# Split weights kept in DRAM by the first token block, x1 and weight stores issued by Pool, and column-tile products whose tiles end one by one

## The chip, the cores and the metric

The kernel runs on one core of one Trainium2 chip. The metric is device time in microseconds of one execution. A core has TensorE (PE in the profile, with its weight loads as PEld), VectorE (DVE), ScalarE (ACT), GpSimd (POOL) and SyncE (SP, which here only issues DMAs). Each engine works off its own queue of instructions in order; semaphores order them among each other. DMAs move data between DRAM and the on-chip SBUF.

## The reference

One layer, sequence 2048, model width 1024, all in float32:

```
h = rmsnorm(x, norm1_w);  p = h @ w_in
y_ssd = ssd_mixer(p[z, xBC, dt])     # causal conv over 4 steps + silu on x, B, C; chunked scan; gate; norm
y_ml  = mlstm_mixer(p[qk, v, o, i, f])  # causal conv + silu on q, k; exponential gates; matrix memory; norm
x = x + concat(y_ssd, y_ml) @ w_out
x = x + hier_moe(rmsnorm(x, norm2_w))   # top-1 of 4 groups, top-2 of 8 experts in it, SwiGLU experts
out = rmsnorm(x, norm_f_w)
```

`w_in` is 1024 rows wide (13 products of 512 columns here, and a few gate columns), `w_out` has 2048 rows and 1024 columns.

## The kernel before, in words

The mixer goes over the sequence in four token blocks of 512 tokens (`for b in range(nblk)`, L1112), some 510 us each; after the last, from about 2100 us on, come the experts, which stream all expert weights. In each block `product` (L260) is called 13 times for `w_in` and 8 times for halves of `w_out` quarters.

A product has four accumulators of 128x512 in PSUM (`acc`). To keep float32 accuracy with a faster matmul form, each operand is a sum of a high and a low half, and a product is three passes: high by high, low by high, high by low. The activations' halves (`hh`, `hl`) are made once per block. The weights' halves are made for each product anew, by `wpieces` (L244): a piece is 256 rows by 512 columns, one DMA on SP of 512 KB into `raw` (two buffers), then for each 128 rows `split` (L233): ScalarE rounds to `whi` (L239 or L236) and VectorE subtracts to `wlo` (L240 or L237). `whi` and `wlo` have five buffers each. A `w_in` product has four pieces, a half of a `w_out` quarter two: 68 pieces per block, 272 in all. Each piece feeds 24 matmuls: 4 accumulators x 2 row groups x 3 passes, one accumulator's 6 after another's.

There are two kinds of product. Kind "t" puts tokens on the accumulators' rows; kind "c" puts columns there, so that each accumulator is one column tile, and `conv` (L282) takes each tile through the causal convolution: a copy to `craw` on ScalarE (L288), small copies of the history on Pool (L287, L289), a scaled copy (L294), three multiply-adds on VectorE (L301), a tanh (L302) and a last step on VectorE (L303), which makes `xc` (x, B and C) or `qk`. PE transposes `xc` to `tx` (L1160), and multiplies `qk` to `sp` (L1287). The scans (`ssd_scan`, L1170, and the mLSTM's) alternate between PE, VectorE, ScalarE and Pool. Seven products of a block are of kind "c".

At a block's end `x1`, the residual sum, is stored twice to DRAM: as it is (`accd`), and after Pool has multiplied it in place by `norm2_w` (`scaled`, L610) as `x1d`. `stores` (L597) issues these eight DMAs of 512 KB on SP, in the next block's start. The tile of `x1` is loaded with the next block's `x` (2 MB, L1366, on SP) when they are done with it.

The queues are not written by hand: the tile framework schedules all instructions from the dependences, the buffers (a buffer is taken again when its last reader is done) and hints such as `tc.issue_after`; `side` steps are handed out between the accumulators of a product. So an edit moves instructions far from its own lines.

The core of the split, L239 and L240:

```
A.activation(hi, src, AF.Copy, scale=w)
V.scalar_tensor_tensor(lo, src, w, hi.bitcast(F32), op0=OP.mult, op1=OP.subtract)
```

## Time and profile before

| | |
|---|---|
| median of 3 runs | 2999.13 us (2998.03 to 3005.5) |
| profiled execution | 3002.55 us |
| its span | 3000.7 us |
| mean granted clock of TensorE | 0.977 |
| PE busy | 2809.5 us, 94% |
| DVE busy | 2135.3 us, 71% |
| ACT busy | 1485.5 us, 50% |

The span is the stretch that the profiler saw; the execution's own time lies 1.85 us above it. Busy times are sums of an engine's instructions; a wait is idle time of an engine, put down to the instruction of another engine that ended it. The granted clock is TensorE's clock as the throttle let it run, as a share of full speed. SP is not counted as busy, since it only issues.

### The profile page before, as it was taken

The numbers are of one execution on the slowest core, as the hardware profiler recorded it, in microseconds if no ns is written. First come the engines' busy times: TensorE is split into PE (matmuls) and PEld (weight loads), VectorE is DVE, ScalarE is ACT, GpSimd is POOL, SyncE is SP. The second block draws the span as 40 slices with busy tenths as digits, with TensorE's granted clock in tenths as the row PEclk, the third lists the DMA queues.
The fourth block names the chain that finished last, engine by engine and source line by source line (L and its number), as shares of the span: only waits on it lengthen the run. The fifth ranks groups of instructions, "written<-read, shape, count | busy, mean of one in ns | idle before, by whom it ended". The sixth has DMA issues, their size and how long they took to land. (4 is left out here: it accounts for less than half of the span.)

```text
span 3000.7 us, 41203 instructions
## 1 busy us (share of the span) xinstructions
PE 2809.5 (94%) x13444; PEld 2226.4 (74%) x13444; DVE 2135.3 (71%) x4035; ACT 1485.5 (50%) x2326; POOL 666.8 (22%) x721
## 2 busy tenths in 40 slices
PE   7999999999999999999999999996889899999985
PEld 5778877777887777788777788785667677787763
DVE  6886487688658678856767974775787777757773
ACT  5544345454434544544445453433666666646662
POOL 1431010352101045100006510001122322412433
PEclk9999999999999999999999999997999999999997
DMA  4222322422322241232224133143998999878983
GB/s 150 70 64 92 91 78 76 145 68 75 95 71 78 84 155 57 71 99 91 65 73 152 57 99 92 54 119 135 310 321 281 311 295 302 277 238 261 302 291 95
DMA packets 228917, 438.05 MB, mean 146 GB/s; under 512 B 38218, under 2 KB 38294, under 8 KB 228641
## 3 DMA queue, kind: packets, MB, share of 16 engines
q1 hardware_dynamic: 206640, 380.88, 38.6%
q0 software_dynamic: 22000, 53.75, 6.7%
q8 instruction: 142, 2.33, 0.3%
q14 instruction: 135, 1.10, 0.1%
HBM read 400.84 MB, written 54.95 MB: 152 GB/s over the span
## 5 line engine op out<-in xcount | busy, mean ns | idle before, releaser
L643 DVE TENSOR_TENSOR lo<-mraw,hi 128x1024 fp32r<-128x1024 f32 x384 | 454.9, 1230 | 75.0 <-ACT hi L642 60.6
L239 ACT ACTIVATE whi<-raw,pcol 128x512 fp32r<-128x512 f32 x416 | 295.0, 721 | 344.0 <-PE acc L277 140.1
L240 DVE SCALAR_TENSOR_TENSOR wlo<-raw,pcol,whi 128x512 fp32r<-128x512 f32 x416 | 318.5, 781 | 201.0 <-ACT whi L239 200.2
L642 ACT CAST hi<-mraw 128x1024 fp32r<-128x1024 f32 x384 | 384.0, 1051 | 87.7 <-DMA mraw<-in_exp_w_up_dram 34.9
L275 PE MATMUL acc<-hh,whi 128*128 128x512 f32 x896 | 366.6, 410 | 0.6 <-ACT whi L239 0.6
L275 PE MATMUL acc<-hh,wlo 128*128 128x512 f32 x896 | 357.6, 401 | 8.1 <-DVE wlo L240 7.9
L275 PE MATMUL acc<-hl,whi 128*128 128x512 f32 x896 | 360.4, 402 | 0.0
L277 PE MATMUL acc<-whi,hh 128*128 128x512 f32 x768 | 311.0, 405 | 2.0 <-ACT craw L288 2.0
L277 PE MATMUL acc<-whi,hl 128*128 128x512 f32 x768 | 310.2, 404 | 0.0
L277 PE MATMUL acc<-wlo,hh 128*128 128x512 f32 x768 | 308.6, 404 | 0.0
L277 PE MATMUL acc<-whi,mh 128*128 128x512 f32 x512 | 204.5, 399 | 0.0
L275 PEld LDWEIGHTS acc<-hh,wlo 128*128 128x128 f32 x896 | 169.3, 189 | 47.0 <-DVE wlo L240 10.9
L277 PE MATMUL acc<-whi,ml 128*128 128x512 f32 x512 | 203.4, 397 | 0.0
L277 PE MATMUL acc<-wlo,mh 128*128 128x512 f32 x512 | 203.1, 398 | 0.0
L289 POOL COPY hist<-craw 128x3 f32<-128x3 f32 x112 | 39.0, 349 | 718.5 <-ACT craw L288 718.1
L275 PEld LDWEIGHTS acc<-hh,whi 128*128 128x128 f32 x896 | 170.2, 190 | 34.3 <-issue 3.5
L275 PEld LDWEIGHTS acc<-hl,whi 128*128 128x128 f32 x896 | 169.9, 190 | 32.0 <-issue 2.6
L287 POOL COPY craw<-hist 128x3 f32<-128x3 f32 x112 | 69.1, 620 | 479.4 <-DVE ir L426 360.5
L277 PEld LDWEIGHTS acc<-whi,hh 128*128 128x128 f32 x768 | 146.1, 190 | 35.7 <-ACT craw L288 3.8
L277 PEld LDWEIGHTS acc<-wlo,hh 128*128 128x128 f32 x768 | 145.7, 190 | 34.9 <-issue 1.9
L277 PEld LDWEIGHTS acc<-whi,hl 128*128 128x128 f32 x768 | 146.4, 191 | 31.8 <-issue 1.0
L809 POOL DMA_INDIRECT accd<-pv,eti x46 | 85.5, 1859 | 338.9 <-ACT hi L642 102.2
(421 smaller groups left out, 6156.8 us busy)
## 6 DMA issues: line engine op xcount, KB each, us to landing
raw<-in_w_in_dram SPq DMA_DIRECT2D x208, 512.0 KB
mraw<-in_exp_w_gate_dram SPq DMA_DIRECT2D x128, 512.0 KB
mraw<-in_exp_w_up_dram SPq DMA_DIRECT2D x128, 512.0 KB
mraw<-in_exp_w_down_dram SPq DMA_DIRECT2D x128, 512.0 KB
raw<-in_w_out_dram SPq DMA_DIRECT2D x64, 512.0 KB
xi<-in_x_dram SPq DMA_DIRECT2D x16, 512.0 KB
x<-in_x_dram SPq DMA_DIRECT2D x4, 2048.0 KB
accd<-x SPq DMA_DIRECT2D x16, 512.0 KB
```

Source lines behind the costliest of these rows:

```text
L239: A.activation(hi, src, AF.Copy, scale=w)
L240: V.scalar_tensor_tensor(lo, src, w, hi.bitcast(F32), op0=OP.mult, op1=OP.subtract)
L275: mm = PE.matmul(acc[i], b[:, s], a, start=f, stop=e)
L277: mm = PE.matmul(acc[i], a[:, s], b, start=f, stop=e)
L287: G.tensor_copy(raw[:, 0:3], hist[:, ct, :])
L289: h = G.tensor_copy(hist[:, ct, :], raw[:, T:T + 3])
L642: A.copy(hi, raw)
L643: V.tensor_tensor(lo, raw, hi.bitcast(F32), op=OP.subtract)
L809: return G.indirect_dma_start(out=accd, out_offset=bass.IndirectOffsetOnAxis(ap=en[0], axis=0), in_=pvs[t], in_offset=None, bounds_check=S ...
```

## The change

In the first block, `wpieces` loads a piece as two DMAs of 256 KB into two smaller tiles `raw` (two buffers), splits each into its part of one tile `wsp` of 128 x 2 x 2 x 512 (1 MB; three buffers), and Pool stores that tile to a DRAM tile of its own (`keep`, called one piece later). In the later blocks a piece is one DMA of 1 MB on SP from there into `wsp`, and `split` is not called. The stores of `x1` of the blocks 0 to 2 are issued by Pool; the last block's by SP. In a product of kind "c" the first half of the rows goes piece by piece as before; the last two pieces are taken together, and each accumulator gets its 12 matmuls in one go. The number of `side` steps stays the same.

```diff
--- before.py
+++ after.py
@@ -41,7 +41,6 @@
 LAST = '.H.Kd.e.PgQ.tA..B..C..ua.D.b', 'HvKwdepxgq'
 NQ = 4
 FIRST, START = 5, 10
-WB = 5
 
 
 def bc(ap, shape):
@@ -239,20 +238,36 @@
             A.activation(hi, src, AF.Copy, scale=w)
             V.scalar_tensor_tensor(lo, src, w, hi.bitcast(F32), op0=OP.mult, op1=OP.subtract)
 
-    loads = []
+    loads, kept, pend = [], {}, []
+
+    def keep():
+
+        for o, t in pend:
+            G.dma_start(o, t.bitcast(F32))
+        pend.clear()
 
     def wpieces(w, r0, nk, c0, scale=None):
 
+
         for kp in range(nk // 2):
-            raw = wp.tile([128, 2, T], F32, name="raw", tag="raw")
             a = r0 + kp * 256
-            loads.append(nc.sync.dma_start(raw, w[a:a + 256, c0:c0 + T].rearrange("(k p) c -> p k c", p=128)))
+            both = wp.tile([128, 2, 2, T], F32R, name="wsp", tag="wsp", bufs=3)
+            if (w.name, a, c0) in kept:
+                loads.append(nc.sync.dma_start(both.bitcast(F32), kept[w.name, a, c0]))
+            else:
+                raws = []
+                for k in range(2):
+                    raw = wp.tile([128, T], F32, name="raw", tag="raw")
+                    loads.append(nc.sync.dma_start(raw, w[a + k * 128:a + k * 128 + 128, c0:c0 + T]))
+                    raws.append(raw)
+                for k in range(2):
+                    sw = None if scale is None else pcol[:, scale + 2 * kp + k:scale + 2 * kp + k + 1]
+                    split(both[:, k, 0], both[:, k, 1], raws[k], sw)
+                keep()
+                o = kept[w.name, a, c0] = dram.tile([128, 2, 2, T], F32, name="w%d" % len(kept))
+                pend.append((o, both))
             for k in range(2):
-                hi = wp.tile([128, T], F32R, name="whi", tag="whi", bufs=WB)
-                lo = wp.tile([128, T], F32R, name="wlo", tag="wlo", bufs=WB)
-                sw = None if scale is None else pcol[:, scale + 2 * kp + k:scale + 2 * kp + k + 1]
-                split(hi, lo, raw[:, k, :], sw)
-                yield 2 * kp + k, hi, lo
+                yield 2 * kp + k, both[:, k, 0], both[:, k, 1]
 
     def accs():
         return [ps_acc.tile([128, T], F32, name="acc", tag="acc") for _ in range(4)]
@@ -260,10 +275,12 @@
     def product(kind, w, r0, nk, c0, src, scale=None, side=iter(())):
 
 
+
         acc = accs()
         ps = wpieces(w, r0, nk, c0, scale)
-        for k0 in range(0, nk, 2):
-            two = [next(ps), next(ps)]
+        n0 = nk // 2 if kind == "c" else nk
+        for k0 in [*range(0, n0, 2)] + [n0] * (n0 < nk):
+            two = list(islice(ps, 2 if k0 < n0 else nk - n0))
             for i in range(4):
                 s = slice(i * 128, i * 128 + 128)
                 for k, whi, wlo in two:
@@ -276,7 +293,8 @@
                         else:
                             mm = PE.matmul(acc[i], a[:, s], b, start=f, stop=e)
                 with tc.issue_after(mm.ins):
-                    next(side, None)
+                    for _ in two[::2]:
+                        next(side, None)
         return acc
 
     def conv(ps, ct, dest):
@@ -597,7 +615,7 @@
     def stores(o, t0, x1):
         for i in range(4):
             with tc.issue_after(loads[-1].ins):
-                nc.sync.dma_start(o[t0 + i * 128:t0 + i * 128 + 128, :], x1[i] if isinstance(x1, list) else x1[:, i, :])
+                (G if kept and t0 < S - T else nc.sync).dma_start(o[t0 + i * 128:t0 + i * 128 + 128, :], x1[i] if isinstance(x1, list) else x1[:, i, :])
             yield
 
     def scaled(x1, alloc):
@@ -1111,6 +1129,7 @@
     whole(gates2(*g1, gate))
     for b in range(nblk):
         t0 = b * T
+        keep()
         dt, cum, eacs, etot, dec, vs, enm = gate
 
         def hsrc(k, hs=hs):
```

Per engine, over the program: PE has the same 20394 instructions; VectorE and ScalarE have 408 fewer each; Pool issues 68 weight stores and 24 x1 stores more; SP issues 136 raw loads of half the size in place of 272, and 204 loads of 1 MB, and 24 stores fewer. The weight tiles take the same room in SBUF, 28 KB per partition (before 2 x 4 KB of `raw` and 10 x 2 KB; after 2 x 2 KB and 3 x 8 KB).

The first place is SP at the start of block 1, before. `x_604` is the tile of x1 that block 0 leaves, `x_5072` the same tile with block 1's x; in brackets is what a DMA waits for.

```order
L249 DMA raw<-in_w_in_dram 128x2x512 [waits DMAHW6_49,DVE_49]
L600 DMA accd<-x_604 128x1024
L249 DMA raw<-in_w_in_dram 128x2x512 [waits DMAHW2_49,DMAHW7_49,DVE_49,Activation_49]
L600 DMA accd<-x_604 128x1024 [waits DMAHW3_49]
L600 DMA accd<-x_604 128x1024 x2
L600 DMA x1d<-x_604 128x1024 [waits Pool_49] x2
L600 DMA x1d<-x_604 128x1024 [waits DMAHW0_49,Pool_49]
L600 DMA x1d<-x_604 128x1024 [waits DMAHW1_49,Pool_49]
L249 DMA raw<-in_w_in_dram 128x2x512 [waits DMAHW2_49,DVE_49,Activation_49]
L249 DMA raw<-in_w_in_dram 128x2x512 [waits DMAHW3_49,DVE_49]
L1366 DMA x_5072<-in_x_dram 128x4x1024 [waits DMAHW5_49,DMAHW4_49,DMAHW6_49,DMAHW1_49,DMAHW7_49,DMAHW0_49,PE_49]
```

After, at the same place: `w_...` are the kept pieces, `x_5108` is block 1's x.

```order
L256 DMA wsp<-w_429 128x2048 [waits DMASW4_49,DMASW3_49,DMASW5_49,DMASW2_49,DMASW6_49,DMASW1_49,DMASW7_49,DMASW0_49,PE_49]
L625 DMA n_5249<-in_norm_w_dram 128x512 [waits DVE_49]
L625 DMA n_5255<-in_norm_w_dram 128x512 [waits DVE_49]
L256 DMA wsp<-w_464 128x2048 [waits DMASW3_49,DMASW5_49,DMASW0_49,PE_49]
L256 DMA wsp<-w_499 128x2048 [waits DMASW4_49,DMASW6_49,DMASW1_49,PE_49]
L256 DMA wsp<-w_510 128x2048 [waits DMAHW4_49,PE_49]
L256 DMA wsp<-w_626 128x2048 [waits DMAHW7_49,DMAHW2_49,PE_49]
L1385 DMA x_5108<-in_x_dram 128x4x1024 [waits DMASW4_49,DMASW5_49,DMASW3_49,DMASW6_49,DMASW2_49,DMASW7_49,DMASW1_49,DMAHW3_49,DMASW0_49,Pool_49]
L256 DMA wsp<-w_668 128x2048 [waits DMAHW0_49,PE_49]
L256 DMA wsp<-w_717 128x2048 [waits DMAHW5_49,DMAHW1_49,PE_49]
L256 DMA wsp<-w_728 128x2048 [waits DMAHW6_49,DMAHW2_49,PE_49]
```

The stores of x1 have left SP, the load of x waits for Pool (whose queue has the eight stores, with eight multiplies between them) and stands ahead of `w_668`.

The second place is PE in block 1, in the product of X1, of kind "c", before: `acc_5523` and `acc_5524` are two of its accumulators, the other matmuls are of the first scan.

```order
L275 MATMUL acc_5523<-hh_4165,whi_5630 128x512
L275 MATMUL acc_5523<-hl_4166,whi_5630 128x512
L275 MATMUL acc_5523<-hh_4165,wlo_5631 128x512
L1205 MATMUL pS_5419<-xe_5417,bn0_5116 128x512
L1207 MATMUL pi_5421<-st_200,ct0_5046 128x512
L275 MATMUL acc_5523<-hh_4165,whi_5634 128x512
L275 MATMUL acc_5523<-hl_4166,whi_5634 128x512
L275 MATMUL acc_5523<-hh_4165,wlo_5635 128x512
L275 MATMUL acc_5524<-hh_4165,whi_5630 128x512
L275 MATMUL acc_5524<-hl_4166,whi_5630 128x512
L275 MATMUL acc_5524<-hh_4165,wlo_5631 128x512
L275 MATMUL acc_5524<-hh_4165,whi_5634 128x512
L1185 MATMUL ar_5436<-br1_208,selA_111 128x256
L275 MATMUL acc_5524<-hl_4166,whi_5634 128x512
```

After, the same product's last accumulator is `acc_5529`; `acc_5715` belongs to the next product, Z0.

```order
L292 MATMUL acc_5529<-hh_4225,wsp_5582 128x512
L292 MATMUL acc_5529<-hl_4226,wsp_5582 128x512
L292 MATMUL acc_5529<-hh_4225,wsp_5582 128x512 x2
L292 MATMUL acc_5529<-hl_4226,wsp_5582 128x512
L292 MATMUL acc_5529<-hh_4225,wsp_5582 128x512
L292 MATMUL acc_5529<-hh_4225,wsp_5584 128x512
L292 MATMUL acc_5529<-hl_4226,wsp_5584 128x512
L292 MATMUL acc_5529<-hh_4225,wsp_5584 128x512 x2
L292 MATMUL acc_5529<-hl_4226,wsp_5584 128x512
L292 MATMUL acc_5529<-hh_4225,wsp_5584 128x512
L294 MATMUL acc_5715<-wsp_5719,hh_4223 128x512
L294 MATMUL acc_5715<-wsp_5719,hl_4224 128x512
```

An accumulator gets 12 matmuls in a row where it got 6.

The third place is PE at the first transposes of X1's tiles (`tx`), in the product of Z0, before: the product of X1 stands 76 rows ahead, with much of the scan between.

```order
L277 MATMUL acc_5746<-whi_5787,hh_4163 128x512
L277 MATMUL acc_5746<-whi_5787,hl_4164 128x512
L277 MATMUL acc_5746<-wlo_5788,hh_4163 128x512
L277 MATMUL acc_5743<-whi_5817,hh_4165 128x512
L1160 MATMUL tx_5677<-ident_103,xc_5663 128x128 x4
L1160 MATMUL tx_5697<-ident_103,xc_5683 128x128 x4
L277 MATMUL acc_5743<-whi_5817,hl_4166 128x512
L277 MATMUL acc_5743<-wlo_5818,hh_4165 128x512
L277 MATMUL acc_5743<-whi_5821,hh_4165 128x512
L277 MATMUL acc_5743<-whi_5821,hl_4166 128x512
L277 MATMUL acc_5743<-wlo_5822,hh_4165 128x512
```

After, the rows that follow directly on the last rows shown above:

```order
L294 MATMUL acc_5715<-wsp_5719,hh_4223 128x512 x2
L294 MATMUL acc_5715<-wsp_5719,hl_4224 128x512
L294 MATMUL acc_5715<-wsp_5719,hh_4223 128x512
L294 MATMUL acc_5716<-wsp_5719,hh_4223 128x512
L294 MATMUL acc_5716<-wsp_5719,hl_4224 128x512
L294 MATMUL acc_5716<-wsp_5719,hh_4223 128x512 x2
L294 MATMUL acc_5716<-wsp_5719,hl_4224 128x512
L1179 MATMUL tx_5649<-ident_103,xc_5635 128x128 x4
L1179 MATMUL tx_5669<-ident_103,xc_5655 128x128 x4
L294 MATMUL acc_5716<-wsp_5719,hh_4223 128x512
L294 MATMUL acc_5717<-wsp_5719,hh_4223 128x512
L294 MATMUL acc_5717<-wsp_5719,hl_4224 128x512
```

The transposes stand 11 matmuls of Z0 behind the last of X1, and those of X1's first tile 35 product matmuls behind the end of that tile.

## Rows read from the trace of the kernel before

**Rows 1.** the page, part 1: busy time of each engine.

```profile
PE 2809.5 (94%) x13444; PEld 2226.4 (74%) x13444; DVE 2135.3 (71%) x4035; ACT 1485.5 (50%) x2326; POOL 666.8 (22%) x721
```

**Rows 2.** windows by block: length; busy (x) of PE, PEld, DVE, ACT, POOL; PEclk; DMA; GB/s.

```profile
30.00:545.00 515.00, 502.12 (x2472) 402.37 (x2470) 367.14 (x782) 238.10 (x416) 82.42 (x102) 0.99 0.26 80
545.00:1055.00 510.00, 493.94 (x2428) 396.61 (x2428) 367.32 (x812) 232.75 (x405) 105.00 (x119) 0.99 0.28 88
1055.00:1565.00 510.00, 494.25 (x2438) 396.66 (x2436) 368.21 (x813) 233.91 (x407) 104.65 (x119) 0.99 0.28 88
1565.00:2060.00 495.00, 477.91 (x2334) 385.86 (x2333) 352.03 (x776) 212.22 (x362) 104.63 (x115) 0.99 0.32 99
```

**Rows 3.** waits of PE in blocks 1 to 3: total us, times, longest.

```profile
PE acc L275 <- DVE wlo L240: 7.9, 4, 2.5
PE tx L1160 <- DVE xc L303: 7.4, 4, 2.4
PE sp L1287 <- DVE qk L303: 7.2, 3, 2.5
PE tk L1297 <- DVE mm L1289: 6.1, 6, 1.5
PE py L1199 <- DVE m L1193: 3.6, 4, 1.2
PE ar L1185 <- DVE sg L1189: 3.1, 3, 1.1
```

**Rows 4.** waits of PE in block 0: total us, times, longest.

```profile
PE tx L1160 <- DVE xc L303: 3.5, 2, 2.4
PE sp L1287 <- DVE qk L303: 2.1, 1, 2.1
```

**Rows 5.** windows just after two waits of PE, columns as in rows 2.

```profile
574.00:577.40 3.40, 3.20 (x8) 2.55 (x9) 3.34 (x6) 0.63 (x1) 1.34 (x2) 0.50 0.57 114
652.50:655.90 3.40, 3.40 (x9) 2.67 (x8) 2.48 (x4) 1.80 (x4) 2.10 (x2) 0.50 0.49 134
```

**Rows 6.** lines of the four blocks: busy us, mean ns, idle before and releaser.

```profile
L239 ACT ACTIVATE whi<-raw,pcol 128x512 fp32r<-128x512 f32 x411 | 291.6, 721 | 344.0 <-PE acc L277 140.1 <-PE acc L275 119.0 <-DMA raw<-in_w_in_dram 78.0
L240 DVE SCALAR_TENSOR_TENSOR wlo<-raw,pcol,whi 128x512 fp32r<-128x512 f32 x411 | 314.9, 781 | 201.0 <-ACT whi L239 200.2
L236 ACT CAST whi<-raw 128x512 fp32r<-128x512 f32 x128 | 78.7, 620 | 144.5 <-PE acc L277 104.7 <-DMA raw<-in_w_out_dram 21.4 <-PE acc L275 16.6
L237 DVE TENSOR_TENSOR wlo<-raw,whi 128x512 fp32r<-128x512 f32 x128 | 86.9, 687 | 89.4 <-PE acc L277 38.8 <-ACT whi L236 38.5 <-PE acc L275 12.0
```

**Rows 7.** window around one 512 KB weight load issued at 302.0, columns as in rows 2.

```profile
302.00:303.00 1.00, 1.00 (x6) 0.79 (x5) 0.00 (x0) 0.46 (x1) 0.00 (x0) 1.00 0.02 4
303.00:305.40 2.40, 2.40 (x12) 1.93 (x11) 0.69 (x1) 0.21 (x2) 0.00 (x0) 1.00 0.58 217
```

**Rows 8.** timeline of SP's queue at the start of block 1: start, us.

```profile
574.23 0.37 SPq L249 DMA_DIRECT2D raw<-in_w_in_dram  x1
574.65 2.22 SPq L600 DMA_DIRECT2D accd<-x  x3
576.91 11.18 SPq L600 DMA_DIRECT2D x1d<-x  x4
588.20 1.24 SPq L249 DMA_DIRECT2D raw<-in_w_in_dram  x2
```

**Rows 9.** window of products alone, line L277: us, PE busy (x) and PEld busy (x).

```profile
300.40:355.90 55.50, 55.50 (x239) 44.70 (x239) 1.00 0.34 104
```

**Rows 10.** lines of POOL: busy us, mean ns, idle before.

```profile
L590 POOL DMA_INDIRECT lst<-ent,sl x36 | 45.6, 1267 | 8.0 <-issue 6.4 <-DVE xc L301 1.0 <-DVE bt L301 0.5
L610 POOL TENSOR_TENSOR x<-x,n 128x512 f32<-128x512 f32 x24 | 31.9, 1358 | 10.9 <-DMA accd<-x 10.8
```

**Rows 11.** the page, part 2: GB/s in 40 slices of 75 us.

```profile
GB/s 150 70 64 92 91 78 76 145 68 75 95 71 78 84 155 57 71 99 91 65 73 152 57 99 92 54 119 135 310 321 281 311 295 302 277 238 261 302 291 95
```

**Rows 12.** window of the scan stretch of block 1, columns as in rows 2.

```profile
600.00:730.00 130.00, 123.65 (x593) 95.63 (x593) 113.72 (x209) 61.97 (x104) 59.84 (x59) 0.99 0.23 67
```

## The prediction

> **What bounds the kernel now.** I read the totals first. TensorE is busy 94% of the span, VectorE 71%, ScalarE 50% [rows 1]: nothing is gained by taking work from ScalarE or VectorE unless TensorE stops waiting for them. Then the windows by token block: in each block of some 510 us TensorE is idle 12.9, 16.1, 15.8 and 17.1 us (515.00 − 502.12, and so on) at a granted clock of 0.99 [rows 2]. The four blocks offer 62 us of idle time plus what the clock loses, and no more, since the matmuls stay the same in number and shape. The second half of the span, the experts, moves 238 to 321 GB/s where the blocks move 54 to 157 [rows 11], and the change doesn't touch it.
>
> Next, who ends the idle time in blocks 1 to 3. Six groups make 35.3 of the 48.9 us there [rows 3], and VectorE is named in all: 7.9 us for `wlo`, the low half of a split weight; 7.4 for `xc` ahead of the transposes `tx` and 7.2 for `qk` ahead of the scores `sp`, both last steps of the convolutions; 12.8 inside the two scans (`tk`, `py`, `ar`). Block 0 has the same two convolution waits, 5.6 us [rows 4]. The cause is in the scan stretch: VectorE is busy 113.72 of 130 us there, 87%, while TensorE reaches 123.65 [rows 12].
>
> [...]
>
> **The change part by part, blocks 1 to 3.** Each piece of weights arrives split. Per block 104 `whi` and 104 `wlo` of one kind and 32 of the other go: the `wlo` are 104 × 781 + 32 × 687 ns = 103 us of VectorE, the `whi` 104 × 721 + 32 × 620 ns = 95 us of ScalarE [rows 6]. VectorE falls from 367 to about 264 us per block. On the path that sets the end this is worth what TensorE waited:
> - `wlo`: all 7.9 us, since the instruction is gone.
> - `tx` and `sp`, 14.6 us: they fall due when VectorE has worked off its queue, and 103 of 367 us of that queue, over a quarter, were `wlo`. The products of kind "c" finish their four column tiles one by one, 12 matmuls apart in place of 6, so the first convolutions start earlier against the last matmul: 36, 24 and 12 matmuls ahead in place of 18, 12 and 6, at 55.50 / 239 = 0.232 us each [rows 9] 4.2 us earlier for the first. Bounds: nothing (the order only moves `tx` closer, as it did before) and all 14.6. In the new order 35 product matmuls (8.1 us) stand between the end of X1's first tile and its transposes, so I am near the upper end and take 0.8, 11.7 us.
> - the scans' 12.8 us: chains through VectorE with dependences of their own; a shorter queue shortens only the queueing part. Bounds 0 and 12.8; I take half, 6.4 us.
> - the clock: three stretches at `wlo` and four of the five others, 7 × 1.7 = 11.9 us.
>
> Together 37.9 us. In exchange come loads of 1 MB. One 512 KB load gave no data in its first microsecond (4 GB/s) and was done 3.4 us after its issue [rows 7]. A 1 MB load is then between 3.4 us (were size free) and 1.0 + 2 × 2.4 = 5.8 us. A slot comes free when TensorE is done with a piece, and there are three slots, so a load has two pieces of 24 × 0.232 = 5.6 us, 11.1 us, to land; where a "c" product holds its last two pieces together it is 1.25 pieces, 7.0 us, since both come free only during the last tile's 12 matmuls. 5.8 is under 7.0: I cost the loads at nothing inside a block. What hides them is the product itself, and it stops hiding them if something stands ahead of the load on SP.
>
> **The start of a block.** Before, SP's queue was blocked by stores: it issued one at 574.65 and the four x1d stores, each waiting for Pool's multiply, until 588.20, and two weight loads stood behind them for 13.5 us [rows 8]. Moved to Pool these leave SP. But the 2 MB load of x for this block, into the same tile, now waits for Pool's stores of it, and stands on SP ahead of the load of a later weight piece (`w_668`). Pool issues 8 stores and 8 multiplies there: no plain store is on Pool before, so I take the nearest row, 1267 ns for an indirect one, and 1358 ns per multiply [rows 10]: 8 × 2.6 = 21 us, and 3.4 us until the last landed. So the x load is issued some 24 us after the first store, and `w_668` right behind it. TensorE has five pieces ahead of that weight, 5 × 5.6 = 28 us. `w_668` lands 3.4 us after its issue if the x load costs it nothing (in time), and 6.5 us later if it goes behind all 2 MB of it (at 321 GB/s [rows 11]), some 34 us after the first store: 0 to 6 us late. Other matmuls stand between the five pieces and x shares the engines, so I take 2, in three block starts +6 us.
>
> [...] With the shorter lead of the new slots, stores left on SP would have cost up to 13.5 − 7.0 = 6.5 us at each of three starts, an estimate.
>
> **Block 0.** Nothing is removed here. Raw weights come in two loads of 256 KB into two tiles (before two tiles of 512 KB, so half the room), and Pool writes each split piece out, 68 stores of 1 MB. A raw tile's cycle is load, `whi`, `wlo`: at most 3.4 + 0.72 + 0.78 = 4.9 us [rows 6, 7] against 5.6 us of a piece, so it fits, with 0.7 us to spare and VectorE's queue not counted. A split tile is free again after its product and its store; the store is issued one piece later and has some 8 us. Per piece 0.5 MB come and 1 MB goes in 5.6 us, 283 GB/s at the most, under the 321 that the experts' part reaches [rows 11]. Bounds: 0, and every piece late by 1.5 us (VectorE two operations behind), 68 × 1.5 = 102 us. The nearest row, the cycle that fits, says near 0; I take a wait like the ones in rows 3 (2.4 + 1.7 us) twice, +8 us. The finishing of "c" tiles one by one helps `tx` and `sp` here too, 5.6 us and three stretches of clock, 5.1 us; without relief for VectorE I take half, −5.
>
> **Into the experts.** The last weight loads are 1 MB among the first expert weights: +2 us.
>
> **Sum.** −37.9 + 6 + 8 − 5 + 2 = −27 us against the profiled execution, 3002.55 us (its span is 3000.7). That execution is 3.4 us above the median of 2999.13, so the forecast is 3002.55 − 27 − 3.4 = 2972 us. Its own range: with all waits and all clock of blocks 1 to 3 gone and no cost, −49 − 8 → 2942; with half of the gain (−22) and costs of 20 → 2997.
>
> **Rivals.**
> 1. *Everything goes.* A queue on VectorE shorter by over a quarter might let every chain run ahead: all 62 us of idle time and 11 stretches of clock (19 us), −81 → 2918. For it: VectorE ends every one of the waits in rows 3. Against it: `tk`, `py` and `ar` are short waits in many places, as chains of their own make them.
> 2. *No change.* The gaps move: the order is laid out anew by a scheduler, which before put `tx` right behind the work it waits for, and SP's queue now stalls on the x load. 4 us at each of three starts, each with 1.7 us of clock, and block 0's costs of 16 use up most of the gain: 17 + 16 = 33 of 38, which is 2990 to 3008. For it: the lead of a 1 MB load is 7.0 us at worst, that of a 512 KB load before was larger. Against it: idle time that VectorE ended is twice that sum.
> 3. *Slower: block 0 is paced by the raw tiles.* With two 256 KB tiles the next load can't be issued before VectorE's `wlo`, and VectorE has 87% of its time taken in the scans [rows 12]. If two operations of 0.7 to 0.8 us are ahead of each `wlo`, the cycle is 4.9 + 1.5 = 6.4 us, and with the store's share of the DMA engines some 6.8, against 5.6: 1.2 × 68 = 82 us. −38 + 6 + 82 + 2 − 3.4 → 3051. It decides from 0.5 us per piece on, where 34 us eat the gain. Against it: in the scans a piece takes longer than 5.6 us, since other matmuls stand between, and three split tiles lend 11 us of lead.
>
> [...]
>
> **How the numbers follow.** Forecast 0.54, rival 1 0.13, rival 2 0.16, rival 3 0.17. Under 0.3%, 9 us either way (2990 to 3008), a measurement of this kernel can't be told from no change. Faster: 0.52 of the forecast, rival 1 and 0.01 of rival 2, 0.66. Same: 0.02 of the forecast and 0.13 of rival 2, 0.15. Slower: rival 3 and the rest of rival 2, 0.19. The range takes in the forecast's own, rival 2 and the near ends of the other two: 2930 to 3020.
>
> **What would show it.** Right: in the windows of blocks 1 to 3 VectorE near 264 us, TensorE's idle time near 8 us each, no wait for `wlo`, `tx` and `sp` mostly gone, a few waits for DMA `wsp` at block starts. Wrong: waits for DMA `wsp` inside the blocks (1 MB loads take over 7 us); block 0 longer than 515 us with ScalarE's `whi` waiting for `raw` (rival 3); `tx` and `sp` as long as before (the order ate the relief); the experts' part of another length.

## The result, and the profile after

The changed kernel takes 3020.32 us (median of 8 runs, 3007.56 to 3024.21) against 3001.15 us: the ratio is 1.0059, 95% interval 1.0045 to 1.0074. It is slower by 18 us by the ratio (19 by the medians) where 27 us of gain were forecast, and its runs lie further apart than those of the kernel before. Its profiled execution took 3019.25 us, its span is 3017.5.

The page's part 1 and the windows of the changed kernel, to be read against [rows 1, 2] (the windows follow its own block starts; after the times come PE, PEld, DVE, ACT, POOL, then the granted clock, DMA share, GB/s):

```profile
PE 2814.2 (93%) x13444; PEld 2227.0 (74%) x13444; DVE 1878.1 (62%) x3627; ACT 1229.1 (41%) x1918; POOL 680.4 (23%) x813
```

```profile
30.00:560.00 530.00, 498.19 (x2412) 394.84 (x2411) 364.41 (x763) 230.04 (x403) 116.31 (x171) 0.98 0.60 213
560.00:1067.00 507.00, 494.45 (x2430) 397.40 (x2429) 280.99 (x675) 147.85 (x270) 97.83 (x128) 0.99 0.46 159
1067.00:1575.00 508.00, 493.66 (x2428) 396.83 (x2427) 281.27 (x675) 147.62 (x269) 98.48 (x127) 0.99 0.46 159
1575.00:2068.00 493.00, 481.40 (x2348) 388.11 (x2348) 265.90 (x633) 131.57 (x230) 95.39 (x121) 0.99 0.48 163
```

VectorE and ScalarE lost the work that was meant to go: 257 and 256 us of busy time over the span. TensorE didn't follow. In the first block it is idle 31.8 us in place of 12.9; in the three others together 38.5 in place of 48.9.

For a ledger I divide each trace at the first product matmul of each block (there are 6528, 1632 per block). The "rest" is the span after the last. What comes before block 0, some 26 us, is left out.

| profiled execution | block 0 | block 1 | block 2 | block 3 | rest |
|---|---|---|---|---|---|
| before | 509.2 | 510.3 | 509.2 | 496.1 | 949.5 |
| changed | 533.7 | 507.1 | 508.3 | 493.0 | 948.9 |

Block 0 lost 24.5 us; the blocks that read the kept weights gained 3.2, 0.9 and 3.1. The experts' part is the same. The lengths are those of one execution each: *stores_on_act* below, which differs from the changed kernel in block 0 alone, has 505.8, 505.2 and 492.7 us in the later blocks, so a single length is good to some 3 us.

The clock has a part in it. By the clock records of the traces TensorE's stretches at a granted clock of 0.50 (these records hold 0.50 and 1.00 and no other value; in the kernel before the matmuls of a product start 0.43 us apart at 0.50, from 574.8 on, and 0.23 apart at 1.00, from 578.5 on) grew in block 0 from 10.2 to 20.5 us, which, counted as half the speed, costs 5.1 us more; the rest of the 24.5 is idle time. In blocks 1 to 3 together they grew from 27.2 to 34.1 us.

**Where block 0 went.** The waits of TensorE there (against [rows 4]; total us, times, longest):

```profile
PE tx L1179 <- DVE xc L321: 8.7, 4, 3.3
PE ib L1310 <- DVE msg L1301: 3.9, 1, 3.9
PE tm L1243 <- DVE ml L1247: 3.9, 2, 3.6
PE ar L1204 <- DVE sg L1208: 2.7, 1, 2.7
...
PE acc L292 <- ACT wsp L238: 1.8, 1, 1.8
```

Hardly any of it is a wait for weights. (`ib` is a matmul of the mLSTM's scan; `tm` are transposes of the scan's result ahead of `w_out`, which ScalarE and VectorE split into `mh` and `ml`.) But ScalarE's queue tells another story. Its halves of the split in block 0, before (two lines) and after (two lines), with what ended its idle time ahead of them:

```profile
L239 ACT ACTIVATE whi<-raw,pcol 128x512 fp32r<-128x512 f32 x103 | 73.3, 721 | 93.7 <-PE acc L277 38.3 <-PE acc L275 32.9 <-DMA raw<-in_w_in_dram 17.5
L236 ACT CAST whi<-raw 128x512 fp32r<-128x512 f32 x32 | 19.7, 620 | 35.3 <-PE acc L277 25.4 <-DMA raw<-in_w_out_dram 5.2 <-PE acc L275 4.0
```

```profile
L238 ACT ACTIVATE wsp<-raw,pcol 128x512 fp32r<-128x512 f32 x100 | 71.4, 721 | 124.8 <-DMA raw<-in_w_in_dram 91.8 <-PE acc L292 19.1 <-PE acc L294 11.6
L235 ACT CAST wsp<-raw 128x512 fp32r<-128x512 f32 x32 | 19.4, 620 | 40.7 <-DMA raw<-in_w_out_dram 22.6 <-PE acc L294 17.3 <-PE tm L1243 0.8
```

ScalarE stood 114 us waiting for raw loads where it stood 23. Before, the split waited for a free buffer (PE); now it waits for data. ScalarE works in order, so what stands behind such a split is late too. Its timeline in the changed kernel, and two rows of VectorE's (start, us, in brackets the idle time and who ended it):

```profile
283.98 0.72 ACT L238 ACTIVATE wsp<-raw,pcol 128x512 fp32r<-128x512 f32 x1 [1.22 <-DMA raw<-in_w_in_dram]
287.24 0.72 ACT L238 ACTIVATE wsp<-raw,pcol 128x512 fp32r<-128x512 f32 x1 [2.54 <-DMA raw<-in_w_in_dram]
287.87 1.25 ACT L1246 ACTIVATE mh<-tm,pcol 128x512 fp32r<-128x512 f32 x2
```

```profile
287.99 0.75 DVE L239 SCALAR_TENSOR_TENSOR wsp<-raw,pcol,wsp 128x512 fp32r<-128x512 f32 x1 [2.51 <-ACT wsp L238]
288.66 1.40 DVE L1247 SCALAR_TENSOR_TENSOR ml<-tm,pcol,mh 128x512 fp32r<-128x512 f32 x2
```

The two `mh` could not start until the split had its load; the low half and `ml` on VectorE follow, and TensorE, which needs the PSUM tile that `mh` and `ml` read, waits for `ml` 3.6 us (the longest `tm` above). The wait is named after VectorE; its origin is a load two engines away.

**Where the gain of the later blocks went.** The waits of TensorE in blocks 1 to 3, against [rows 3]:

```profile
PE ib L1310 <- DVE msg L1301: 11.4, 3, 3.8
PE tx L1179 <- DVE xc L321: 10.7, 7, 2.7
PE pr L557 <- DVE pre L555: 10.3, 3, 3.8
...
PE sp L1306 <- DVE qk L321: 0.6, 3, 0.2
```

`wlo` is gone, as are nearly all of `sp`, `tk`, `py` and `ar`. In their place stand one long `ib` and one long `pr` (a matmul of the routing) per block, 11.4 us where 1.0 was and 10.3 where 2.0 was, and `tx` got longer. How `pr` comes about is seen on VectorE's and Pool's timelines (VectorE first):

```profile
572.81 0.31 DVE L504 TENSOR_TENSOR lg<-l,r 128x144 f32<-128x144 f32 x1
573.15 3.46 DVE L505 TENSOR_TENSOR lg<-lg,rb 128x144 f32<-128x144 f32 x1
576.65 0.17 DVE L510 MAX8 mx<-lg 128x8 f32<-128x8 f32 x1
```

```profile
573.31 1.31 POOL L628 TENSOR_TENSOR x<-x,n 128x512 f32<-128x512 f32 x1
574.55 0.56 POOL L618 DMA_DIRECT2D x1d<-x  x1
575.13 1.31 POOL L628 TENSOR_TENSOR x<-x,n 128x512 f32<-128x512 f32 x1
```

An addition that takes 0.31 us (the median of the line's four) took 3.46: it ended when Pool's second multiply did (576.44). With the stores on Pool, its multiplies of x1 come earlier than before and fall beside the routing steps. How it was held the trace doesn't show: by its rows, of which Pool's spans are rough, the addition began 0.16 us ahead of the first multiply, and it was held past that multiply's end (574.62) to the end of the second.

The DMAs of the changed kernel (KB each, median us from issue to landing):

```profile
wsp<-w SPq DMA_DIRECT2D x204, 1024.0 KB, 4.9
w<-wsp POOLq DMA_DIRECT2D x68, 1024.0 KB, 5.3
...
raw<-in_w_in_dram SPq DMA_DIRECT2D x104, 256.0 KB, 3.0
```

The 1 MB loads land in 4.9 us, within the 3.4 to 5.8 of the prediction, and TensorE waited for one of them 0.5 us in all. SP's queue at the start of block 1, against [rows 8]:

```profile
552.50 24.50 SPq L256 DMA_DIRECT2D wsp<-w  x4
584.73 0.38 SPq L1385 DMA_DIRECT2D x<-in_x_dram  x1
593.64 116.51 SPq L256 DMA_DIRECT2D wsp<-w  x16
```

No store stands there any more. The x load waited for Pool's stores until 584.7, but the next weight load was issued 9 us after it only, and TensorE hardly waits for one (0.5 us above): nothing was late for it.

### The profile page after: what moved, and what is told of

Its sections match the earlier page's. It is cut to its first block, busy times and chain, and to the rows that moved or that the text cites. A ratio compares the mean times of both kernels' runs of the same rounds, so it can differ in the third digit from the quotient of the medians.

```text
span 3017.5 us, 40208 instructions
## 1 busy us (share of the span) xinstructions
PE 2814.2 (93%) x13444; PEld 2227.0 (74%) x13444; DVE 1878.1 (62%) x3627; ACT 1229.1 (41%) x1918; POOL 680.4 (23%) x813
## 3 DMA queue, kind: packets, MB, share of 16 engines
q0 software_dynamic: 35248, 137.64, 13.4%
## 5 line engine op out<-in xcount | busy, mean ns | idle before, releaser
L292 PE MATMUL acc<-hh,wsp 128*128 128x512 f32 x1792 | 607.8, 407 | 2.0 <-ACT wsp L238 1.8
L294 PE MATMUL acc<-wsp,hh 128*128 128x512 f32 x1536 | 505.1, 402 | 0.0
L292 PEld LDWEIGHTS acc<-hh,wsp 128*128 128x128 f32 x1792 | 337.5, 191 | 73.7 <-issue 6.0
L292 PE MATMUL acc<-hl,wsp 128*128 128x512 f32 x896 | 362.2, 404 | 0.0
L294 PE MATMUL acc<-wsp,mh 128*128 128x512 f32 x1024 | 336.5, 399 | 2.7 <-ACT v L1291 2.0
L294 PEld LDWEIGHTS acc<-wsp,hh 128*128 128x128 f32 x1536 | 289.8, 190 | 65.9 <-DVE wsp L239 0.7
L294 PE MATMUL acc<-wsp,hl 128*128 128x512 f32 x768 | 307.1, 400 | 0.0
L294 PEld LDWEIGHTS acc<-wsp,mh 128*128 128x128 f32 x1024 | 191.6, 188 | 46.8 <-ACT v L1291 2.4
L294 PE MATMUL acc<-wsp,ml 128*128 128x512 f32 x512 | 203.2, 397 | 0.0
L292 PEld LDWEIGHTS acc<-hl,wsp 128*128 128x128 f32 x896 | 171.2, 191 | 33.2 <-issue 2.6
## 6 DMA issues: line engine op xcount, KB each, us to landing
mraw<-in_exp_w_gate_dram SPq DMA_DIRECT2D x128, 512.0 KB, 6.9
mraw<-in_exp_w_up_dram SPq DMA_DIRECT2D x128, 512.0 KB, 6.8
mraw<-in_exp_w_down_dram SPq DMA_DIRECT2D x128, 512.0 KB, 5.6
xi<-in_x_dram SPq DMA_DIRECT2D x16, 512.0 KB, 6.2
```

The source lines that it names most:

```text
L292: mm = PE.matmul(acc[i], b[:, s], a, start=f, stop=e)
L294: mm = PE.matmul(acc[i], a[:, s], b, start=f, stop=e)
```

## The experiments

Times are medians with the ratio to the kernel before, run on the same chip. Block lengths are those of the profiled executions, taken as above.

**What is in block 0: the order, the raw tiles, or the stores?** *no_c_split* is the changed kernel with "c" products as before. What it takes away, the last two pieces of a "c" product taken together, is called the c split from here on:

```diff
-        n0 = nk // 2 if kind == "c" else nk
+        n0 = nk
```

> The changed kernel with kind "c" products as before (every piece on its own, six matmuls per accumulator at a time); kept weights and Pool's stores stay. Theory R (in block 0 the two small raw tiles pace the loads, and ScalarE and VectorE, which work in order, stand behind the split that waits for its load): block 0 stays 18 to 27 us longer than in the kernel before, ScalarE's idle time ahead of its half of the split ended by raw DMAs stays near 110 us there. Theory C (the new order of the c products costs the time in block 0): block 0 comes back to within 6 us of the kernel before. For blocks 1 to 3, of which the change gained 6.5 us: without the split the wait for tx should be longer by 2 to 4 us per block if the split was worth anything, and the time 5 to 12 us above the changed kernel.

3015.28 us, 1.0053 [1.0040, 1.0067]; blocks 541.6, 503.8, 502.8, 489.2. Theory C falls: without the new order block 0 is longer still, by 7.9 us (and longer than theory R's range). And I was wrong on the later blocks: they get shorter without it, by 3.3, 5.5 and 3.8 us. The finishing of tiles one by one costs 12.6 us there, which the prediction had down as a gain; measured against the later blocks of *stores_on_act* it is 7.9 us, so 8 to 13. The traces show in what form: without the c split the stretches at half clock in blocks 1 to 3 are 17.0 us long in place of 34.1, which is worth 8.5 us, and TensorE's idle time is 33.5 us in place of 38.5.

*small_raw_all* keeps no weights: all blocks split, with block 0's small raw tiles, the c split and Pool's stores of x1; *small_raw_stores0* adds block 0's stores, never read back:

```diff
 small_raw_all
-                keep()
-                o = kept[w.name, a, c0] = dram.tile([128, 2, 2, T], F32, name="w%d" % len(kept))
-                pend.append((o, both))
...
-                (G if kept and t0 < S - T else nc.sync).dma_start(...)
+                (G if t0 < S - T else nc.sync).dma_start(...)
 small_raw_stores0
-            if (w.name, a, c0) in kept:
+            if False:
...
+                if (w.name, a, c0) not in kept:
...
```

> The changed kernel without any kept weights: all four blocks load raw weights in two 256 KB loads into two small tiles and split them into the three wsp tiles, and nothing is stored. Theory R (small raw tiles pace block 0): every block is 15 to 25 us longer than in the kernel before, 3055 to 3100 us in all, with ScalarE waiting about 110 us per block for raw loads. Theory S (Pool's 68 stores of 1 MB, their issue on Pool and their traffic, cost block 0 its time): block 0 is back within 5 us of the kernel before, 2990 to 3010 us in all.

> As the one without kept weights, but block 0's split weights are stored to DRAM by Pool as in the changed kernel, and never read. Its difference to the one without stores is the cost of the stores alone, in block 0. Theory R: under 5 us. Theory S: 18 to 27 us. If both have a part, each between.

3024.27 us, 1.0084 [1.0070, 1.0098], blocks 513.2, 512.2, 513.6, 505.3; and 3042.34 us, 1.0147 [1.0131, 1.0162], blocks 534.2, 511.5, 512.0, 506.1. In block 0 all that isn't the keeping (small raw tiles and c split) costs 4 us, where my theory R said 15 to 25, and the stores cost 21.0. Theory S has block 0 right, but not the time, which is above its 2990 to 3010. With the changed kernel these two are steps of one ledger, by the ratios: what isn't the keeping (small tiles, c split, Pool's stores of x1) +25 us, the weight stores +19, reading back −26, each good to some 5. Reading the split weights back pays for having stored them and little more.

*half_stores0* stores the high halves only, *stores_on_act* is the changed kernel with the weight stores on ScalarE's queue:

```diff
 half_stores0 (against small_raw_stores0)
-            G.dma_start(o, t.bitcast(F32))
+            G.dma_start(o, t[:, :, 0].bitcast(F32))
...
 stores_on_act (against the changed kernel)
-            G.dma_start(o, t.bitcast(F32))
+            nc.scalar.dma_start(o, t.bitcast(F32))
```

> As the run with small raw tiles in all blocks and block 0's weights stored but never read, but only the high halves are stored: 68 stores of 512 KB, half the bytes and as many instructions. Theory RS: the cost of the stores in block 0, 21.0 us (534.2 against 513.2), falls to 5 to 13 us. Rival Q: it stays 18 to 24 us.

> The changed kernel with the 68 weight stores issued by ScalarE in place of Pool. Theory RS: the traffic is the same and ScalarE's queue gets 68 instructions more; block 0 stays at 528 to 540 us. Rival Q (Pool's queue): block 0 falls to 512 to 518 us, as without stores.

3041.91 us, 1.0140 [1.0125, 1.0156], block 0 532.1; and 3047.55 us, 1.0157 [1.0141, 1.0174], block 0 562.6. Half the bytes cost 18.9 us in place of 21.0, so the cost doesn't go with the bytes, against theory RS. It could go with the packets: the two have the same 35248 in Pool's DMA queue, 128 per weight store, of 4 KB in place of 8. And the stores cost more from ScalarE's queue, where rival Q had them cost nothing. That alone doesn't clear Pool's queue, since on ScalarE the stores stand in the order of the engine that splits. A raw load lands later still there than the 3.0 us of the changed kernel:

```profile
raw<-in_w_in_dram SPq DMA_DIRECT2D x104, 256.0 KB, 4.2
```

The loads beside the stores take 3.0 us with Pool as the issuer and 4.2 with ScalarE, though the stores themselves land alike, in 5.3 and 5.2 us. Whether it is the queue or the moments at which the stores are issued isn't shown.

*stores0_fixed_source* takes the stores' data from a tile that never changes, so that no store waits for a split and none holds a slot; *stores0_two_late* issues each store one piece later:

```diff
 stores0_fixed_source (against small_raw_stores0)
-            G.dma_start(o, t.bitcast(F32))
+            G.dma_start(o, bc(wg.rearrange("p k c -> p (k c)")[:, None, :].bitcast(F32), [128, 4, T]))
...
 stores0_two_late (against small_raw_stores0)
-        for o, t in pend:
+        while len(pend) > 1:
+            o, t = pend.pop(0)
...
```

> As the run with small raw tiles in all blocks and 68 stores of 1 MB in block 0 (never read), but each store's source is a tile that doesn't change (the gate weights, repeated), so that a store waits for no split and holds no wsp slot. Theory W (the stores cost block 0 its 19 to 21 us by their waits: Pool, in order, stands before a store until VectorE's low half is done, 114 us plus 61 us of such waits, and Pool's scan steps and convolution copies stand behind it; or the slot is free later): block 0 falls from 534.2 to 513 to 518 us. Theory X (by being in flight: a raw load takes 3.6 in place of 2.8 us from issue to split whenever a store shares the DMA engines, and the split stands in ScalarE's and VectorE's order): block 0 stays 528 to 536.

> The same with the split tile as the source, but each store is given to Pool one piece later still, so that Pool waits less for a split and the slot is held longer. If the cost is Pool's waiting in order: block 0 from 534.2 to 515 to 525 us. If it is the slot: 538 us or more. If it is the traffic (theory X): within 4 us of 534.

3096.88 us, 1.0316 [1.0302, 1.0331], block 0 583.0; and 3044.10 us, 1.0148 [1.0133, 1.0164], block 0 531.4. Theory W falls with the first: with no waits and no slots held the stores cost 70 us, not 0. The second, in which Pool waits less for a split, is 2.8 us off the 534.2, as theory X has it. The first is far outside theory X's range as well, and the windows of block 0 say why (columns as above):

```profile
30.00:200.00 170.00, 139.05 (x601) 106.79 (x600) 108.82 (x196) 68.43 (x117) 62.82 (x82) 0.90 0.74 270
200.00:350.00 150.00, 123.73 (x520) 93.85 (x520) 87.61 (x157) 50.37 (x84) 44.09 (x58) 0.93 0.78 286
350.00:465.00 115.00, 114.88 (x565) 93.75 (x564) 60.35 (x122) 43.66 (x74) 3.98 (x11) 1.00 0.29 90
```

Waiting for nothing, Pool issued all stores in the first 317 us, and the DMA share is 0.74 to 0.78 until 350; after them TensorE is idle 0.12 us in 115. That by itself proves little, since the kernel before is as busy in the stretch that does this work (280 to 395 us, 563 matmuls, 0.13 us idle), but it puts the whole loss into the time in which stores are in flight. Two things set these stores apart from the real ones: they are crowded, and as their source is a repeated tile, each has 256 packets of 4 KB in place of 128 of 8 (43952 in Pool's DMA queue in place of 35248). Which of the two makes 70 us out of 21 isn't shown.

**The way in which they cost.** I paired each raw issue on SP with its split on ScalarE and took the median time between, over the splits ahead of which ScalarE stood idle. Over seven kernels with two raw tiles and the c split block 0 goes with it: 2.82 us and 513.2 us without stores; 3.53 and 531.4 (two late), 3.54 and 533.7 (changed), 3.62 and 532.1 (half), 3.62 and 534.2 (full); 4.38 and 562.6 (ScalarE's queue); 4.83 and 583.0 (fixed source). (Without the c split, in another order, 3.62 and 541.6.) A raw tile is taken again when its low half is done, so the cycle is that time + 0.72 + 0.75 + 0.15 us between them: 4.4 us without stores, 5.2 with, against 5.6 us of a piece. So the cycle fits with stores too, by its medians. What costs is likely the spread: in the changed kernel three low halves in ten begin 1.2 us or more after their high half (the median is 0.12), and added to 5.2 us that makes a cycle longer than a piece, which it doesn't when added to 4.4. To show that this is the way and no companion, the raw loads need a lead. The first tries were not clean.

*big_raw_fine_slots* has two raw tiles of 512 KB and pays with split tiles of 128 rows, five of them, c products as before; *fine_raw* has four raw tiles of half the width in the same room, *fine_raw_no_c* the same with c products as before:

```diff
 big_raw_fine_slots (against no_c_split)
-            both = wp.tile([128, 2, 2, T], F32R, name="wsp", tag="wsp", bufs=3)
+            raw = wp.tile([128, 2, T], F32, name="raw", tag="raw")
...
+                both = wp.tile([128, 2, T], F32R, name="wsp", tag="wsp", bufs=5)
...
 fine_raw (against the changed kernel)
-                    raw = wp.tile([128, T], F32, name="raw", tag="raw")
+                    for q in range(2):
+                        raw = wp.tile([128, T // 2], F32, name="raw", tag="raw", bufs=4)
...
```

> Kept weights and Pool's x1 stores, c products as before; the room is cut otherwise: raw tiles of 512 KB (two, as in the kernel before) and five wsp tiles of 128 rows each (512 KB) in place of three of 256 rows; so 136 stores of 512 KB in block 0 and 408 loads of 512 KB after it. Theory RS (the stores lengthen a raw load from 2.8 to 3.6 us, and with two small raw tiles the cycle load, high half, low half, 5.2 us and VectorE's queue, then has no slack against 5.6 us of a piece): with a lead of a whole piece the longer load is hidden; block 0 falls from 541.6 us (without the c split) to 509 to 516, the blocks after it stay near 504, 503 and 489, and the time is 2976 to 2992 us, faster than both kernels. Rival Q (the stores cost by their issue on Pool, 0.53 us each, with Pool's steps of the scans behind them): twice as many stores, block 0 at 540 us or above, 3010 to 3040 us. Rival T (the traffic slows everything that moves, whatever the lead): block 0 530 to 540.

> The changed kernel, but in block 0 a raw tile is 128x256 (128 KB), four of them in the same room, and each is split on its own; stores as in the changed kernel. Theory RL (block 0's time follows from the latency of a raw load: issue to split 2.8 us without stores and 513 us, 3.6 with stores of either size and 532 to 534, 4.4 with stores on ScalarE's queue and 563; since a tile's cycle of latency and two halves of the split is held by two tiles per piece): with four tiles the cycle per piece is about 3.6 + 0.4 + 0.4 = 4.4 us in place of 5.2, as it was without stores, so block 0 falls from 533.7 to 511 to 519 us, ScalarE's waits for raw from 114 us to 60 or less, and the time to 2998 to 3008 us. Rival Q2 (the stores cost in another way, by Pool's queue or by the slots that they hold): block 0 stays at 530 to 536 us or longer, as the halves add 136 instructions each on ScalarE and VectorE.

> The same with the c products as before. Theory RL: block 0 from 541.6 to 511 to 522 us, the later blocks as without the c split (504, 503, 489), 2985 to 3000 us in all, the first version that beats the kernel before. Rival Q2: block 0 538 to 545, 3012 to 3018 us.

3015.86 us, 1.0047 [1.0034, 1.0059], block 0 530.1 (541.6 in *no_c_split*): 11.5 of the 32 us came back. 3027.93 us, 1.0088 [1.0075, 1.0102], block 0 546.9; and 3023.77 us, 1.0086 [1.0071, 1.0101], block 0 542.3. All three miss: each comes out in the range of its rival (T for the first, Q2 in block 0 for the others). They change more than the lead, since a split of 256 columns takes ScalarE 502 ns where 512 take 721, 21 us more for `w_in` in block 0 (92.4 after 71.4), and with the five fine slots there are 136 stores of 512 KB, so by an estimate from *half_stores0* (128 packets in such a store) twice the packets. So they speak against the way above without refuting it, and the next pair has to decide.

The clean pair takes the room from the conv input tiles. *craw2* has two of these in place of four, and *craw2_raw4* four raw tiles besides:

```diff
 craw2 (against the changed kernel)
-        raw = tmp.tile([128, T + 3], F32, name="craw", tag="craw", bufs=4)
+        raw = tmp.tile([128, T + 3], F32, name="craw", tag="craw", bufs=2)
...
 craw2_raw4 (against craw2)
-                    raw = wp.tile([128, T], F32, name="raw", tag="raw")
+                    raw = wp.tile([128, T], F32, name="raw", tag="raw", bufs=4)
```

> The changed kernel with two conv input tiles (craw) in place of four. It is the control for the next one, which needs their room: expected within 8 us of the changed kernel, block 0 at 530 to 542 us, since a conv tile may wait for the one two before it.

> The same, and in the room that is free four raw tiles of 256 KB in place of two, so that raw loads are issued a piece earlier; stores, sizes and instructions are the same. Theory X (the stores lengthen each raw load, and the two raw tiles leave no room for that: over seven kernels block 0 goes with the time from a raw load's issue to its split, 2.8 us 513, 3.5 to 3.6 us 531 to 534, 4.4 us 563, 4.8 us 583): with a piece's lead the lengthened load is hidden, block 0 is 12 to 20 us shorter than in the control, the later blocks within 2 us of it, and ScalarE's waits for raw, 114 us, are halved. Rival (the latency goes along with the cost but isn't its way, for instance the order laid out around the stores, or VectorE and Pool in each other's way): block 0 within 5 us of the control.

3017.35 us, 1.0053 [1.0041, 1.0065], blocks 533.8, 506.3, 505.2, 492.3; and 2995.70 us, 0.9984 [0.9975, 0.9993], blocks 511.6, 506.2, 505.3, 492.6. The lead alone takes 22.2 us out of block 0 (12 to 20 were expected) and nothing anywhere else; block 0 is then no longer than without stores (513.2). ScalarE's split of `w_in` in block 0, control and then lead:

```profile
L238 ACT ACTIVATE wsp<-raw,pcol 128x512 fp32r<-128x512 f32 x100 | 71.0, 720 | 121.6 <-DMA raw<-in_w_in_dram 82.9 <-PE acc L292 20.7 <-PE acc L294 14.8
```

```profile
L238 ACT ACTIVATE wsp<-raw,pcol 128x512 fp32r<-128x512 f32 x98 | 67.7, 717 | 94.4 <-PE acc L294 41.9 <-PE acc L292 40.7 <-DMA raw<-in_w_in_dram 7.6
```

The stores are all there, and the median raw load lands even later (3.4 us for `w_in`), but the split waits for a slot again, as before the change, and for data 7.6 us. That is shown: beside the stores the raw loads come later (3.5 to 3.6 us from issue to split where it is 2.8 without), and two small raw tiles had no room for it. What it is in the stores that makes a load late, their packets, their time in flight or the moment of issue, stays open.

**The stores of x1 and Pool's multiplies.** *x1_on_sp* is the changed kernel with these stores on SP, *before_x1_on_pool* the kernel before with them on Pool:

```diff
 x1_on_sp (against the changed kernel)
-                (G if kept and t0 < S - T else nc.sync).dma_start(...)
+                nc.sync.dma_start(...)
 before_x1_on_pool (against the kernel before)
-                nc.sync.dma_start(...)
+                (G if t0 < S - T else nc.sync).dma_start(...)
```

> The changed kernel with the stores of x1 on SP again. Theory P (moving the stores to Pool put Pool's multiplies beside VectorE's routing steps, which are stretched by them, and PE waits 3.1 to 3.9 us for pre at each of three block starts, with a stretch at half clock behind each): that wait falls to 0.7 us, worth 3 x (2.7 + 1.7) = 13 us, and what comes in its place is a late weight load behind the stores on SP, 3 to 7 us at each start: between 10 us faster and 10 us slower than the changed kernel. Rival (the move is worth nothing either way): within 3 us, with the wait for pre as it was. Block 0 stays as in the changed kernel by theory R and by its rivals.

> The kernel before with only the x1 stores of blocks 0 to 2 moved to Pool. In the changed kernel the move was worth 5 us per block start. Theory L (that worth comes from the short lead of the split tiles' loads, which stood behind the stores on SP): with the longer lead of the raw tiles here it is worth nothing or less, -2 to +10 us in all, as Pool's multiplies fall beside VectorE's routing steps and the wait for pre grows to 3 us. Rival (the stores on SP cost a few microseconds at each start in the kernel before too): 8 to 15 us faster than the kernel before.

3035.97 us, 1.0125 [1.0110, 1.0141], blocks 533.3, 512.2, 511.9, 499.5; and 3014.45 us, 1.0038 [1.0025, 1.0050], blocks 510.4, 513.4, 511.9, 500.4. In the changed kernel the move to Pool is worth 5.1, 3.6 and 6.5 us per start, more in all than the range that I gave (the wait for `pr` does go without it, but `tx` waits 31.2 us in all four blocks where it waited 19.4, and the stretches at half clock in blocks 1 to 3 are 58.1 us long in place of 34.1). In the kernel before, whose loads have the longer lead, the move costs 13 us, a little above theory L's range. Then the multiplies themselves, on VectorE: *before_dve_x1* and *before_x1_pool_dve* start from the kernel before (the second has the stores of x1 on Pool too), *fine_raw_no_c_dve_x1* from *fine_raw_no_c*:

```diff
-                G.tensor_tensor(xh, xh, n2, op=OP.mult)
+                V.tensor_tensor(xh, xh, n2, op=OP.mult)
```

> The kernel before with one edit: x1's multiplies by the norm's weights in blocks 0 to 2 are VectorE's in place of Pool's. Theory P2 (a VectorE operation that meets a Pool tensor operation is stretched until that ends: in the kernel before 3.42 us in place of 0.74 at 567.5, 1.80 in place of 0.75 for a low half at 581.1, and the wait for wlo of 2.5 us at each block start follows from it): the waits for wlo go, 7.9 us and 1.7 us of half clock behind each, 5 to 13 us faster than the kernel before. Rival (VectorE's queue gets 5.5 us longer at each start, and the low halves stand behind it): within 4 us of the kernel before or slower.

> The kernel before with x1's stores of blocks 0 to 2 on Pool and its multiplies on VectorE: it tells whether the 13 us that the stores on Pool cost there came from Pool's multiplies beside VectorE's routing. Theory P2: the wait for pre of 4.0 to 4.7 us at each start goes, and the time is 2988 to 3002 us. Rival (they came from elsewhere, as from the x load that waits for Pool): 3008 to 3018.

> As the last, and the multiplies of x1 by the norm's weights in blocks 0 to 2 are VectorE's (24 of some 0.7 us) in place of Pool's. Theory P2 (in the blocks after the first what is left of the wait for pre, 3.1 to 4.0 us at each start and a stretch of half clock, comes from Pool's multiplies, beside which VectorE's routing steps are stretched from 0.3 to 3.5 us): the wait falls to 1 us or less, 8 to 14 us off in the three later starts. Rival (VectorE does eight multiplies more there, in order, and the routing steps stand behind them): the wait stays within 1 us or grows to 5 us, time within 4 us of the last or slower.

2998.73 us, 0.9995 [0.9986, 1.0004]; 2996.49 us, 0.9983 [0.9974, 0.9992]; 3015.07 us, 1.0057 [1.0043, 1.0071]. The first says that in the kernel before nothing is won that can be told from zero, where 5 to 13 us were expected: the waits for `wlo` leave the list, but `pS`, which waits for Pool, grows from 1.8 to 7.3 us. The second shows that the 13 us of the stores on Pool came from Pool's multiplies: with them on VectorE the same stores cost nothing. In the third the blocks 1 to 3 go from 505.5, 503.1 and 489.0 to 500.5, 499.7 and 487.5 us, 9.9 us, in the expected range, while VectorE does eight multiplies more in each.

**The version without the three causes.** *lead_no_c_dve_x1* keeps the weights and the stores on Pool, and has four raw tiles (two conv tiles), c products as before, and VectorE's multiplies.

> Three findings together: four raw tiles (room from two conv tiles fewer), c products as before, and VectorE in place of Pool for x1's multiplies in blocks 0 to 2; kept weights and the stores on Pool stay. If they add: block 0 at 509 to 516 us, the later blocks at 500, 500 and 488 us as in the run with fine raw tiles and VectorE's multiplies, rest 948 to 953 us: 2968 to 2982 us, 0.6 to 1.1% faster than the kernel before. If the two conv tiles are missed without the c split, or block 0 keeps the 8 us that it was longer without that split: 2983 to 2996.

2973.78 us (2971.74 to 2974.73), ratio 0.9909 [0.9892, 0.9925]: 28 us faster than the kernel before, as much as was forecast for the change. Its blocks take 504.8, 499.3, 499.4 and 487.0 us, the first less than the 509 to 516 expected. Its stretches at half clock in blocks 1 to 3 are 10.2 us long. Its windows and what is left of TensorE's waits in blocks 1 to 3:

```profile
30.00:540.00 510.00, 498.52 (x2466) 399.88 (x2464) 364.01 (x775) 229.29 (x408) 120.92 (x173) 0.99 0.61 224
540.00:1040.00 500.00, 492.38 (x2436) 395.97 (x2436) 279.12 (x688) 147.64 (x270) 87.43 (x119) 0.99 0.46 161
1040.00:1541.00 501.00, 492.59 (x2439) 395.72 (x2438) 279.67 (x688) 147.15 (x269) 88.43 (x121) 1.00 0.46 162
```

```profile
PE acc L294 <- ACT craw L306: 8.8, 6, 2.7
PE tx L1179 <- DVE xc L321: 6.6, 9, 1.4
PE pr L557 <- DVE pre L555: 2.1, 3, 0.7
```

TensorE is idle some 8 us per block, the figure that the prediction gave as the sign of being right. The first wait, for ScalarE's copy into a conv tile, was 1.3 us in the kernel before; it looks like the price of two conv tiles in place of four.

## Why the prediction was wrong

The sum missed in two places of about equal size. Block 0 was costed at +8 − 5 us and took +24.5, 21.5 us more. Blocks 1 to 3 were summed to −37.9 + 6 and gave −7.2, 24.7 us less. The first is a step of the mechanism that failed; the second is two costs that the sum put at a gain or at nothing: the c split, 8 to 13 us there, and Pool's multiplies beside VectorE, 9.9. Term by term:

- *What bounds the kernel*: right. TensorE's idle time and clock in the blocks were what could be won, and the last version wins 28 us.
- *Block 0, costed at +8 − 5 us*: the step that failed is the end "near 0" because "it fits". The mechanism was named as rival 3 (two 256 KB raw tiles pace block 0, "with the store's share of the DMA engines"), but I held a cycle of 4.9 us, with the 3.4 us of a larger load that flew alone [rows 7], against 5.6. The cycle itself was hardly off: beside a store the time from issue to split is 3.5 to 3.6 us, where a small load without stores takes 2.8, and the cycle is 5.2. The error is that a cycle that fits on average was taken to cost nothing. I asked whether the piece is late for TensorE (it hardly ever is, 1.8 us), and not who stands behind the split on ScalarE, an engine that works in a fixed order. "VectorE's queue not counted" stood in the prediction as a remark; it belonged into the sum. Per piece block 0 lost 24.5 / 68 = 0.36 us, under the 0.5 from which rival 3 was to decide; that was enough because the later blocks gained 7 us and not 38.
- *`wlo`, 7.9 us gone*: right, and VectorE's share fell (by 86 us per block in the windows, not 103, since neighbouring operations overlap at their ends: the sum of their durations fell by 301 us over the three blocks, the busy time by 259).
- *`tx` and `sp`, 0.8 of 14.6 us*: half wrong. `sp` went, `tx` grew from 7.4 to 10.7, and `ib` came with 11.4. The c split, put down as a gain of lead, costs 8 to 13 us in blocks 1 to 3 (*no_c_split*) and is worth 7.9 in block 0. Most of the cost is clock (34.1 us at half clock against 17.0); by which instruction it comes was not tried.
- *the scans' chains, half of 12.8*: they gave more than that; `tk`, `py` and `ar` are down to 1.1.
- *loads of 1 MB at nothing, +6 for the x load at the block starts*: the first right (0.5 us of waits for `wsp`), the second too much.
- *the stores of x1 left on SP would have cost up to 6.5 us at each start*: right in size, 3.6 to 6.5, but not for the reason given: without the move TensorE waits 1.5 us for kept weights, and the rest is `tx` and clock (*x1_on_sp*). What I missed is the other side: with the stores moved to Pool, its multiplies fall beside VectorE's routing, `pr` 10.3 us and a stretch at half clock behind each. [Rows 10] gave the multiply's time, and I counted it only as time on Pool.
- *the clock*: in blocks 1 to 3 ten waits are over 2 us, where there were nine, and the stretches at half clock grew by 6.9 us; so in place of 11.9 us won some 3.4 were lost. The 1.7 us per stretch of clock, which the sum and rivals 1 and 2 use, was my estimate, and no run shows it for a stretch by itself: what the trace shows is a granted clock of 0.50 for 3.4 us after each of two waits [rows 5], half of which I took as lost, and what the runs showed in place of seven stretches gone is 34.1 us at 0.50 where there were 27.2.
- *no change of the experts' part*: right, 948.9 us after 949.5.

The three things that were missed are the raw loads' lead, 22.2 us in block 0, the c split, 12.6 in the later blocks, and Pool's multiplies, 9.9: 44.7 in all, and from 3020.3 to 2973.8 us it is 46.5. That the two agree so well is partly luck. By the blocks' lengths the last version gained 28.9 us in block 0, 6.7 more than the lead alone (once it has the lead, block 0 is 6.8 us shorter without the c split, where it was 7.9 longer), and 22.7 in the later blocks; the experts' part, which nothing touched, was 6.6 us longer in its profiled execution.

## What to carry to other kernels

When a transfer is added beside an existing stream, take the stream's load time from a stretch in which both fly, and ask who stands behind the first consumer in its engine's order, not only whether the last one waits. A cycle that fits on average was not free here, on an engine that works in a fixed order: 5.2 us against 5.6, and block 0 20.5 us longer than with 4.4 (533.7 after 513.2). Give such a stream a lead of a whole step before paying for anything else; here 4 KB per partition were worth 22 us. And before work is moved to Pool or brought forward there, look at what VectorE does in the same microseconds; here Pool's multiplies beside it cost 9.9 us in three blocks.
